# One weight buffer more, one load buffer less, and S5 steps held back during attention: a two-layer hybrid backbone on one core

## The chip, the cores and the metric

The kernel runs on 1 core of a Trainium2 chip. The metric is the device time of one execution in microseconds; shown are the median and the spread of several runs. One more execution was taken with the hardware profiler, and all rows below are of that one.

## The reference

One inference step of a hybrid backbone over two layers. 128 context tokens and 128 latent tokens run through the same weights, so the kernel treats them as 256 columns. For each layer:

```
mod = silu(cond) @ w_mod + b_mod                # six vectors of 2048, for context and for latent
h   = rms_norm(x) * (1 + scale1) + shift1
z   = h @ w_in      # q | k | v | rglru x | rglru gate | s5 input | three branch gates
A   = attention(q, k, v)                        # 8 heads, 2 kv heads, QK norm, rotary positions
B   = gelu(gate) * rg_lru(conv4(x))             # both directions
C   = glu(gelu(s5(u) + d*u))                    # complex diagonal scan, both directions, 64 groups
x  += gate1 * ((g0*(A@w_pa) + g1*(B@w_pr) + g2*(C@w_ps)) @ w_o)
a,b = rms_norm(x)*(1+scale2)+shift2 @ w_up
x  += gate2 * ((gelu(conv3(a)) * b) @ w_down)
```

All of it is in float32. The outputs are both token streams, the new keys and values, and the final states of the two recurrences.

## The kernel before, in words

Features lie on the 128 partitions, the 256 tokens along the free dimension. A weight matrix is cut into tiles that give 128 output features each; such a tile is one *item* of kind "w" in a list, with 2048 values per partition, loaded as two halves of 1024 (512 KB each).

**Precision.** TensorE multiplies in a rounded 32-bit form, so each half is split. `emit_split` (L192) copies the raw half into a high part on ScalarE (`whi`), and the closure `small` subtracts that from the raw half on VectorE (`wlo`). Activations are split too. For each 128 rows of the contraction `mmx` (L379) runs one matmul of the high weights over 512 columns (high and low activations) and one of the low weights over 256; a tile has 16 such pairs, in one PSUM bank of two. `joined` (L391) then copies half of the bank on ScalarE and adds the other half on VectorE (`pj`); that add empties the bank, and the tile's evacuation `evac` follows. `unit` (L362) makes such an item; `unit2` (L403) makes one whose two halves are two output tiles with a contraction of 1024, so it has two `pj` (the projections `w_pa`, `w_pr`, `w_ps` and the GLU).

**Buffers.** `emit_dma` (L153) issues a load on SyncE's queue (SP) into one of `NRAW` buffers "raw". Loads are issued in item order, and the program may emit one only when the load `NRAW` places before it has been used (L181). The scheduler below gives it a buffer that has come free, so it waits on the chip for that buffer's last reader. A raw weight half is free after its `wlo`; a raw modulation load after its matmul. In the startup the loads go round `NRAW` raw buffers and eight places in wide tiles that nothing else uses yet; in the feed-forward blocks two of five tiles use wide places E0 and F4 (L160). `whi` and `wlo` have `HLB` buffers each. `nhalf` counts halves that are split and not used up: `emit_split` refuses when it stands at `HLB`, and `spend` (L230), called after the first eight pairs of a tile, gives one back and lets `pump_split` (L299) emit the next. `pump_split` goes no farther than the next weight item. So with three, the second half of the next tile is emitted in the middle of the running tile.

**Modulation.** The 384 modulation loads are read once and multiplied by narrow float32 matmuls straight from the raw buffer (items of kind "mod", `mod_mm` L422, eight records each). 64 of them belong to the startup. The other 320 are spread over the weight items: `filler` adds `MODR[seg]` of a load for each tile and puts in a group of four when the credit reaches four. `seg` is 0 in layer 0 up to the last branch gates, 1 up to its feed-forward, 2 to 4 in the feed-forward of layer 0, 5 in layer 1. Asserts demand that each modulation vector is there before its use.

**Order of the work.** `run_items` (L285) walks through the items. At each weight item it emits loads, splits, the matmuls, the evacuation, and then `feed_att` (L257) and `feed` (L242), which run steps of generators: attention (`att_gen` L1091, one step at each `feed_att`, which also runs in the middle of a tile), the RG-LRU (`lru_gen`, at a rate `RLRU` per tile) and S5 (`s5_gen` L997, in layer 0 with `s5_prep`, which makes the tables). S5 goes last: it gets steps while the planner's clock of VectorE, `clock()`, is below its clock of TensorE, `pe`, plus `LEAD` of the layer (in ns). After each tile `run_items` sets the VectorE clock to at least `pe`, so `LEAD` works afresh for each tile. The planner's costs are the formulas in `tt`, `stt`, `mm` and others; the order they give is in the program, and the framework's scheduler may shift an instruction that is ready ahead of one that is not. Each engine has its own queue of instructions.

S5 starts when half of its input is there (L1253), attention after the value projection (L1328). `pa_begin` drains attention before the projection `w_pa`, and S5 is drained after ten of the sixteen tiles of the third branch gate (`GS0`).

Of the kernel before, what the change touches and what calls it, by code (L numbers as in the profile page):

```python
# [31 lines left out]


class Builder:
    LEAD = (3900, 2700)
    HLB = 3
    GS0 = 10
    PATIENCE = 3
    NRAW = 6
    AHEAD = 20  # L40
    MODR = (1.5, 0.6, 0.65, 0.65, 0.65, 1.2)
    RLRU = (1.9, 1.9)
    NE = (3, 3)
    PA = 1
# [108 lines left out]
    def emit_dma(self, i, extra):  # L153
# [15 lines left out]
        for h in range(len(self.raws.get(i, [])), 2 if w else 1):  # L169
            k = self.nboot % (self.NRAW + 8) - self.NRAW if it.get("boot") else -1  # L170
            if k >= 0:
# [8 lines left out]
            else:  # L180
                if len(self.ring) >= self.NRAW and self.ring[-self.NRAW] not in self.done:  # L181
                    return False
                self.ring.append((i, h))
                raw = self.st("raw", [1024], name="raw", bufs=self.NRAW)
            self.nboot += 1
# [6 lines left out]
    def emit_split(self, i, h):  # L192

        if self.nhalf == self.HLB:
            return False
        self.nhalf += 1
        hi = self.st("whi", [1024], F32R, name="whi", bufs=self.HLB)
        lo = self.st("wlo", [1024], F32R, name="wlo", bufs=self.HLB)
        raw = self.raws[i][h]
# [41 lines left out]

    def feed(self):  # L242

        for g in sorted(self.gens, key=lambda g: g[3] == "s5"):
            if g[3] == "att":
                continue
            s5 = g[3] == "s5"
            g[2] = 0 if s5 else g[2] + g[1]
            if g[4] is not None:
                g[4] += 1  # L250
            while g in self.gens and (self.clock() < self.pe + self.LEAD[self.lay] if s5 else g[2] >= 1):
                if g[4] is not None and g[4] < self.PATIENCE:
                    break
                g[2] -= 1
                self.step(g)
# [1304 lines left out]
    def filler(self, n):  # L1560
        self.credit += self.MODR[self.seg] * n
        while self.credit >= 4 and self.modq:
            self.credit -= 4
            for _ in range(4):
                it = self.modq.pop(0)
                it["ffn"] = self.ffn
                self.items.append(it)
# [135 lines left out]
```

## Time and profile before

| what | value |
|---|---|
| median of 3 runs | 3059.31 us (3058.38 to 3062.9) |
| the profiled execution | 3053.26 us, of it the span 3051.5 us |
| TensorE (PE) busy | 2946.8 us, 97% |
| VectorE (DVE) busy | 2259.1 us, 74% |
| ScalarE (ACT) busy | 1718.7 us, 56% |
| DMA | 723.64 MB, mean 237 GB/s |
| weight splits (`wlo`) | 896, 1095.2 us |
| modulation loads | 384 of 512 KB |

How to read it: all times are microseconds of the profiled execution, counted from its first instruction. A busy share is over the whole span and hides the stages: S5, attention and the RG-LRU run beside the input projection and the branch projections, from about 163 to 820 us in layer 0 and from 1630 to 2230 us in layer 1; the two feed-forward blocks lie behind these. A matmul's end is modelled, so PE busy is not PE at its peak. In a view of waits a row says which engine's instruction sat idle, what it waited for, the idle time in total, how often, and the longest.

### The profile page before, as it was taken

The page shows a single profiled execution, that of the slowest core. Times are in us where ns is not written, and L with a number is a line of the kernel's source. Part 1 is how long each engine was busy: PE and PEld are TensorE (multiplying, and loading weights), DVE is VectorE, ACT ScalarE, POOL GpSimd, SP SyncE. Part 2 cuts the span into 40 slices and gives each one's busy share as a digit, 9 for nine tenths or more (in the row PEclk, how much of TensorE's full clock was granted, in tenths as well). Part 3 has the DMA queues.
Part 4 walks back from the last instruction along what each step waited for, and adds up shares of the span by engine and source line. Part 5 has one row for each costly group of instructions (what it writes and reads, how often), then busy time and mean ns, then how long its engine had stood idle before and what let it go on. Part 6 is the DMA issues. An engine that isn't in the chain of part 4 may idle for free.

```text
span 3051.5 us, 53446 instructions
## 1 busy us (share of the span) xinstructions
PE 2946.8 (97%) x20833; PEld 2474.8 (81%) x20833; DVE 2259.1 (74%) x4000; ACT 1718.7 (56%) x2905; POOL 45.9 (2%) x87
## 2 busy tenths in 40 slices
PE   6899999999999999999999999999999999999999
PEld 4787778777888888888887878777788888888888
DVE  6498888889777878777668787787755777666665
ACT  4355667745456755445567556686345566544553
POOL 0000000000000000000000000000000000000000
PEclk9999999999999999999999999999999999999999
DMA  9866667677776777777776767777677656555553
GB/s 387 308 201 217 236 225 256 238 253 249 242 244 221 251 249 262 257 258 265 250 269 224 261 217 246 252 247 252 240 268 265 210 176 210 191 189 187 185 195 132
DMA packets 188637, 723.64 MB, mean 237 GB/s; under 512 B 21536, under 2 KB 22080, under 8 KB 179552
## 3 DMA queue, kind: packets, MB, share of 16 engines
q1 hardware_dynamic: 180432, 689.86, 66.2%
q0 software_dynamic: 7664, 28.27, 2.5%
q8 instruction: 164, 2.69, 0.3%
q10 hardware_dynamic: 288, 2.10, 0.2%
q14 instruction: 89, 0.73, 0.1%
HBM read 704.46 MB, written 15.68 MB: 236 GB/s over the span
## 4 chain that ended last, share of the span: by engine, by line
PE 68%; DVE 14%; DMA 8%; ACT 7%; issue 3%; ACTq 0%; DVEq 0%; SPq 0%
PE ps_mm L124 60%; DMA raw<-in_w_in 5%; DVE wlo L72 5%; ACT whi L116 3%; PE ps_md L124 3%; PE ps_aux L124 2%; DVE xs L1046 2%; PE ps_v L124 1%; ACT ltmp L112 1%; DMA raw<-in_w_pr 1%; DVE xs L72 1%; PE ps_y L124 1%; DVE pd L72 1%; DMA raw<-in_w_pa 1%; DVE pb L72 1%
## 5 line engine op out<-in xcount | busy, mean ns | idle before, releaser
L124 PE MATMUL ps_mm<-h,whi 128*128 128x512 f32 (+1 forms) x4976 | 1745.2, 395 | 34.5 <-DVE pj L72 26.0
L72 DVE TENSOR_TENSOR wlo<-raw,whi 128x1024 fp32r<-128x1024 f32 x896 | 1095.2, 1223 | 457.4 <-ACT whi L116 448.2
L124 PE MATMUL ps_mm<-h,wlo 128*128 128x256 f32 x4912 | 1342.3, 284 | 18.4 <-DVE wlo L72 18.0
L116 ACT CAST whi<-raw 128x1024 fp32r<-128x1024 f32 x896 | 939.7, 1049 | 544.7 <-PE ps_mm L124 236.6
L124 PEld LDWEIGHTS ps_mm<-h,whi 128*128 128x128 f32 x4976 | 925.8, 190 | 245.8 <-DVE pj L72 31.6
L124 PEld LDWEIGHTS ps_mm<-h,wlo 128*128 128x128 f32 x4912 | 934.6, 190 | 48.8 <-DVE wlo L72 25.8
L116 ACT COPY pj<-ps_mm 128x256 f32<-128x256 f32 x479 | 176.0, 368 | 500.5 <-PE ps_mm L124 499.8
L124 PE MATMUL ps_mm<-hid,whi 128*128 128x512 f32 x1024 | 354.9, 393 | 0.0
L72 DVE TENSOR_TENSOR pj<-ps_mm,pj 128x256 f32<-128x256 f32 x479 | 201.5, 421 | 205.6 <-ACT pj L116 204.9
L124 PE MATMUL ps_mm<-br,whi 128*128 128x512 f32 x896 | 322.8, 402 | 9.8 <-DVE pj L72 8.9
L124 PE MATMUL ps_mm<-hid,wlo 128*128 128x256 f32 x1024 | 277.2, 281 | 0.0
L124 PE MATMUL ps_mm<-br,wlo 128*128 128x256 f32 x896 | 233.4, 281 | 0.7 <-DVE wlo L72 0.6
L124 PEld LDWEIGHTS ps_mm<-hid,whi 128*128 128x128 f32 x1024 | 188.5, 188 | 39.6 <-issue 1.2
L124 PEld LDWEIGHTS ps_mm<-br,whi 128*128 128x128 f32 x896 | 165.5, 188 | 55.3 <-DVE pj L72 18.0
L124 PEld LDWEIGHTS ps_mm<-hid,wlo 128*128 128x128 f32 x1024 | 193.2, 189 | 5.1
L124 PEld LDWEIGHTS ps_mm<-br,wlo 128*128 128x128 f32 x896 | 169.0, 189 | 8.7 <-DVE wlo L72 1.0
L124 PE MATMUL ps_md<-raw,SC 128*32 128x256 f32 x2560 | 160.8, 382 | 0.0
L124 PEld LDWEIGHTS ps_md<-raw,SC 128*32 128x32 f32 x2560 | 78.7, 110 | 56.3 <-issue 15.1
L112 ACT ACT_TABLE_LOAD x81 | 103.9, 1283 | 10.1 <-DMA cv<-in_cT 5.2
L112 ACT ACTIVATE RH<-CST,TINY 128x256 f32<-128x256 f32 x128 | 57.9, 500 | 63.4 <-DVE xs L1046 63.4
L1046 DVE TENSOR_TENSOR_SCAN xs<-RH,xs 128x1056 f32<-128x1056 f32 x32 | 75.3, 2355 | 0.7
L85 DVE SCALAR_TENSOR_TENSOR x<-pj,MOD,x 128x128 f32<-128x128 f32 x192 | 59.0, 349 | 3.1
(239 smaller groups left out, 2434.1 us busy)
## 6 DMA issues: line engine op xcount, KB each, us to landing
raw<-in_w_mod SPq DMA_DIRECT2D x384, 512.0 KB, 6.8
raw<-in_w_in SPq DMA_DIRECT2D x304, 512.0 KB, 4.8
raw<-in_w_up SPq DMA_DIRECT2D x168, 512.0 KB, 4.3
raw<-in_w_down SPq DMA_DIRECT2D x90, 512.0 KB, 4.4
raw<-in_w_up SPq DMA_DIRECT2D x44, 1024.0 KB, 4.8
raw<-in_w_o SPq DMA_DIRECT2D x64, 512.0 KB, 4.4
raw<-in_w_down SPq DMA_DIRECT2D x19, 1024.0 KB, 4.8
raw<-in_w_pa SPq DMA_DIRECT2D x32, 512.0 KB, 4.6
```

The source lines that it names most:

```text
L72: self.nc.vector.tensor_tensor(out=out, in0=a, in1=b, op=op)
L85: self.nc.vector.scalar_tensor_tensor(out=out, in0=a, scalar=s, in1=b, op0=op0, op1=op1)
L112: self.nc.scalar.activation(out, a, func, **k)
L116: self.nc.scalar.copy(out, a)
L124: self.nc.tensor.matmul(out, lhsT, rhs, start=start, stop=stop, **k)
L1046: nc.vector.tensor_tensor_scan(out=x, data0=r, data1=x, initial=0.0, op0=ALU.mult, op1=ALU.add)
```

## The change

`HLB` goes from 3 to 4, so `whi` and `wlo` have four buffers each. `NRAW` goes from 6 to 5. `LEAD` goes from 3900 to 4700 ns in layer 0 and from 2700 to 3300 ns in layer 1, and a new `LEADA` of 1000 ns takes its place in `feed` while an attention generator is alive. `MODR` is 1.3 instead of 1.5 and 1.0 instead of 1.2 in segments 0 and 5, and 0.8 instead of 0.6 to 0.65 in the others. What is computed stays the same.

```diff
--- before.py
+++ after.py
@@ -32,13 +32,14 @@
 
 
 class Builder:
-    LEAD = (3900, 2700)
-    HLB = 3
+    LEAD = (4700, 3300)
+    LEADA = 1000
+    HLB = 4
     GS0 = 10
     PATIENCE = 3
-    NRAW = 6
+    NRAW = 5
     AHEAD = 20
-    MODR = (1.5, 0.6, 0.65, 0.65, 0.65, 1.2)
+    MODR = (1.3, 0.8, 0.8, 0.8, 0.8, 1.0)
     RLRU = (1.9, 1.9)
     NE = (3, 3)
     PA = 1
@@ -241,14 +242,16 @@
 
     def feed(self):
 
+        att = any(g[3] == "att" for g in self.gens)
         for g in sorted(self.gens, key=lambda g: g[3] == "s5"):
             if g[3] == "att":
                 continue
             s5 = g[3] == "s5"
+            lead = self.LEADA if att else self.LEAD[self.lay]
             g[2] = 0 if s5 else g[2] + g[1]
             if g[4] is not None:
                 g[4] += 1
-            while g in self.gens and (self.clock() < self.pe + self.LEAD[self.lay] if s5 else g[2] >= 1):
+            while g in self.gens and (self.clock() < self.pe + lead if s5 else g[2] >= 1):
                 if g[4] is not None and g[4] < self.PATIENCE:
                     break
                 g[2] -= 1
```

## Rows read from the trace of the kernel before

**Rows 1.** The page's head and part 1: span; busy us, share, instructions

```profile
span 3051.5 us, 53446 instructions
...
PE 2946.8 (97%) x20833; PEld 2474.8 (81%) x20833; DVE 2259.1 (74%) x4000; ACT 1718.7 (56%) x2905; POOL 45.9 (2%) x87
```

**Rows 2.** The chain of waits in its last stretch: start us, us, what

```profile
2540.30 507.00 PE ps_mm L124 x2911
```

**Rows 3.** TensorE's waits, whole span: engine line waited for: us, times, longest

```profile
PE ps_mm L124 <- DVE pj L72: 34.9, 29, 4.2
PE ps_mm L124 <- DVE wlo L72: 18.5, 19, 3.6
...
PE ps_mm L124 <- ACT whi L116: 8.5, 11, 1.7
PE ps_aux L128 <- DVE rkc L100: 7.3, 2, 3.7
```

**Rows 4.** TensorE's waits, 0 to 163 us, the startup

```profile
PE ps_mm L124 <- DVE wlo L72: 6.6, 6, 3.6
PE ps_mm L124 <- ACT whi L116: 4.7, 7, 1.1
```

**Rows 5.** TensorE's waits, 163 to 820 us, layer 0 with S5

```profile
PE ps_mm L124 <- DVE pj L72: 18.8, 11, 4.2
```

**Rows 6.** TensorE's waits, 1630 to 2230 us, layer 1 with S5

```profile
PE ps_mm L124 <- DVE pj L72: 13.1, 9, 3.9
```

**Rows 7.** Windows: stretch, us, busy of PE, PEld, DVE, ACT, POOL, clock, DMA

```profile
312.00:500.00 188.00, 177.18 (x1431) 145.49 (x1430) 163.58 (x296) 126.85 (x205) 5.37 (x10) 0.98 0.68 232
1830.00:2005.00 175.00, 168.06 (x1256) 139.51 (x1255) 133.68 (x199) 118.31 (x192) 2.69 (x5) 1.00 0.73 252
```

**Rows 8.** Windows of the tile wlo alone: busy of PE, PEld and DVE

```profile
312.00:500.00 188.00, 100.62 (x373) 71.59 (x372) 56.07 (x46) 0.98 0.68 232
```

**Rows 9.** ScalarE's waits, whole span

```profile
ACT whi L116 <- PE ps_mm L124: 236.6, 188, 6.2
ACT whi L116 <- DMA raw<-in_w_in: 154.5, 108, 6.7
```

**Rows 10.** ScalarE's waits, 163 to 820 us

```profile
ACT whi L116 <- DMA raw<-in_w_in: 63.6, 45, 6.7
...
ACT whi L116 <- PE ps_mm L124: 32.8, 17, 4.9
```

**Rows 11.** VectorE's waits, whole span

```profile
DVE wlo L72 <- ACT whi L116: 448.2, 456, 4.4
```

**Rows 12.** Timeline of TensorE: a modulation group and the tile behind it

```profile
392.97 1.91 PE L124 MATMUL ps_md<-raw,SC 128*32 128x256 f32 x32
394.81 0.50 PE L124 MATMUL ps_mm<-br,whi 128*128 128x512 f32 x1
```

**Rows 13.** Timeline of all engines, 384 to 391 us: start us, us, engine, line

```profile
384.09 0.33 SPq L186 DMA_DIRECT2D raw<-in_w_pa  x1
...
386.49 1.22 DVE L72 TENSOR_TENSOR wlo<-raw,whi 128x1024 fp32r<-128x1024 f32 x1
...
387.73 2.74 SPq L186 DMA_DIRECT2D raw<-in_w_in  x2
387.81 1.05 ACT L116 CAST whi<-raw 128x1024 fp32r<-128x1024 f32 x1
...
388.89 1.23 DVE L72 TENSOR_TENSOR wlo<-raw,whi 128x1024 fp32r<-128x1024 f32 x1 [0.52 <-ACT whi L116]
...
390.22 0.37 ACT L116 COPY pj<-ps_mm 128x256 f32<-128x256 f32 x1 [1.36 <-PE ps_mm L124]
...
390.63 0.42 DVE L72 TENSOR_TENSOR pj<-ps_mm,pj 128x256 f32<-128x256 f32 x1 [0.51 <-ACT pj L116]
```

**Rows 14.** Windows of the tile ps_md alone: busy of PE, PEld, DVE, ACT

```profile
163.00:820.00 657.00, 58.21 (x902) 29.13 (x902) 1.13 (x6) 2.50 (x7) 0.99 0.70 236
1630.00:2380.00 750.00, 61.24 (x968) 30.77 (x968) 1.63 (x8) 1.46 (x4) 0.99 0.72 250
```

## The prediction

> **What bounds the kernel now.** I began with the page's head and its busy line [rows 1]: TensorE is busy for 2946.8 of 3051.5 us, so about 104.7 us are all that any cover of waits can win back. The work itself (448 weight tiles, 384 modulation loads, the S5 matmuls) is the same after the change. The chain of waits shows what a tile costs when nothing disturbs it: in the last stretch 2911 matmuls, 32 to a tile, take 507.00 us, 5.57 us a tile [rows 2]. The chain's DVE and DMA shares elsewhere are not idle TensorE, only the path that happened to arrive last; so the next view was TensorE's own waits [rows 3]. There are few: 34.9 us for the sum that empties a PSUM bank (pj), 18.5 us for the low half of a split weight (wlo), 8.5 us for the high half (whi), 7.3 us for the key norms that open attention (rkc). Cut by stretch, 11.3 us of wlo and whi lie in the startup [rows 4]; of pj, 18.8 us lie in layer 0 while S5 runs [rows 5] and 13.1 us in the same stretch of layer 1 [rows 6]. The two feed-forward blocks have next to none. So the change can matter in some 1250 us, where VectorE carries split, evacuation and S5 steps in one order.
>
> There VectorE is nearly full in layer 0 and not in layer 1: 163.58 us of 188 against 133.68 of 175 [rows 7]. 46 wlo in the first [rows 8], and as many in the second, are 23 tiles, so 7.11 and 5.81 us of VectorE work a tile; the tile's period is 8.17 us in layer 0, and less TensorE's idle 10.82 us (0.47 a tile) it would be 7.70.
>
> **The change, part by part.** Sums are made against the profiled execution, 3053.26 us (1.76 more than its span); the median of the runs is 6.05 above that, and I add it at the end.
>
> Fourth split buffer. With three, the second half of the next tile is split only when TensorE has spent the first half of the running one. With four it may be split half a tile (2.8 us) earlier, and a wait that comes from this gate goes. What it can win is bounded by the 27.0 us of wlo and whi waits [rows 3] and by 0. ScalarE's waits before whi say how much of it is the gate: 236.6 us until TensorE, 154.5 us until a load of the input projection [rows 9]; in layer 0's S5 stretch it is the other way round, 32.8 against 63.6 [rows 10]. I take half: -13.5. VectorE also stops blocking: it sat 448.2 us before wlo until whi [rows 11], with S5 steps and pj queued behind it. Where it runs late it then catches up, so I take a quarter of the pj waits, -9; ends -17 (half) and, as two wlo now can stand ahead of a pj, 32 two-result tiles at up to 0.3 us, +10.
>
> Attention hold. With LEADA at 1000 hardly an S5 step follows a tile while attention lives, as its evacuation and softmax already use that lead. The two waits for rkc are 7.3 us [rows 3]; part of each is its own square root, reciprocal and transpose. I take -4; ends 0 and -7.3.
>
> More lead elsewhere. After each tile the planner fills VectorE until it stands LEAD ahead of TensorE, so 0.8 us more in layer 0 and 0.6 in layer 1 is a larger share per tile, not a larger stock. Layer 0: 7.11+0.8=7.91 us against a tile that needs 7.70; the lower MODR takes 0.2 load a tile away, a quarter of 1.91 us each [rows 12], 0.10, so 7.60. VectorE is over by 0.31 us for some 50 tiles until S5 ends: up to 16 us of new pj waits, less what the fourth buffer gives it back. I take +6; ends 0 and +16. Layer 1: 5.81+0.6=6.41 stays below its period of 7.61: 0. S5 ends earlier in both, and nothing waited for that. Its steps issue DMAs too: tables on POOL's queue in layer 0, blocks on SP's in layer 1, a few tiles later or earlier in either; POOL is idle and SP's are 24 among some 1200: 0.
>
> Five raw buffers. Four modulation loads are issued far ahead of their matmuls and sit in their buffers; before, two buffers went round for weights in that time, now one. One round trip, from issue to the low half, was 6.0 us: issue at 384.09, whi at 387.81, wlo at 388.89 for 1.23; and a load reuses a buffer as soon as its wlo ends (387.71, next issue 387.73) [rows 13]. The tile after a modulation group has two halves, which now come one after the other: 12.1 us from the end of the split before them. The time for it is two tiles, the group (1.91 and some 0.3 to get in) and half a tile, 2.5x5.57+2.2=16.1 us in a calm stage, so that split must end 4.0 us into its tile. In VectorE's queue stand before it, in a tile: 0.41 us until the bank's copy is there (390.22 to 390.63) [rows 13], all its work but the splits, which was 7.11-2.46=4.65 in layer 0 and 5.81-2.46=3.35 in layer 1 and grows by 0.8 and 0.6, and the two wlo themselves (2.46): 8.3 us and 6.8 us. S5's own matmuls lengthen the two tiles by 2x(7.60-5.57-0.72)=2.6 us, with 0.72 for the group spread over its 3.08 tiles. So the half is up to 1.7 us late in layer 0 and 0.2 in layer 1. Groups are 32 records: 902/32=28 in layer 0's stretch and 968/32=30 in layer 1's [rows 14]; at the new rates 24 and 25. The ends are 0 and 24x1.7+25x0.2=+46. The total of weight halves held, five raw and four split against six and three, is the same nine, and an earlier split frees its raw buffer earlier; so I take 0.2 us a group, nearer to nothing: +10. In the pair of loads shown, a start at 384.09 would still give the second half at 396.2, and TensorE reached the second half of the tile behind that group, begun at 394.81 [rows 12], after about 397.6: hidden by 1.4 us. Where it is not hidden, ScalarE's pj copy stands behind the waiting whi, VectorE's pj and S5 steps behind its wlo, and on SP's queue the next loads; TensorE waits for pj then.
>
> The Trainium skill, Perfetto Trace Analysis, section Optimization Strategy, says that the same gap repeating on the engine that should be full can mean that there is no room for the next tile's buffer. By that one adds to the buffer that is waited for, and in layer 0's S5 stretch [rows 10] that is the raw load, of which the change takes one away; it speaks for the slower rival below.
>
> The Trainium skill, DMA: Bandwidth & Descriptors, section Anatomy of one DMA, gives about 2.0 us fixed plus bytes at 436 GB/s, measured on another queue; for 512 KB an estimate of 3.2 us. The row has at most 3.72 (384.09 to 387.81). By the Trainium skill the two trips are about 11.1 us and the lateness in layer 0 is 0.7 us instead of 1.7.
>
> The moved modulation groups are the same 80 and cost the same where they land: 0. One load fewer in flight at the start: 0, ends -2 and +3, as the boot loads also use eight wide places.
>
> Sum: -13.5-9-4+6+10=-10.5, so 3042.8 for a profiled execution and 3048.8 for the median.
>
> **The rivals.** First, forecast: waits for splits and attention shrink, the lead and the raw buffer give part back; 3048.8, its own range 3034 to 3053.
> Second, slower: the single raw buffer beside four parked modulation loads. Place: the second half of the first tile after each group, in both S5 stretches. Price +46; with only the split's -13.5 and attention's -4 beside it +28.5, 3088 at its worst. It decides from (13.5+9+4-6)/49=0.42 us a group on; at twice that, 0.8 a group, the net is 49x0.8-20.5=+18.7, 3078, which I take. For it: ScalarE waits for loads rather than for TensorE in layer 0 [rows 10]. Against: the example is hidden.
> Third, slower: VectorE full in layer 0. +16 for the lead, +5 raw, -6 split, -4 attention: 3070. For it 7.91 over 7.60; against, S5 ends earlier and the tiles after it have VectorE free.
> Fourth, nothing: a wait removed at wlo is taken up at pj, since both stand behind the same VectorE work: 3059. For it: with VectorE at 87%, many pj waits come with no idle VectorE before them.
> Fifth, more: -20 split, -14 pj, -6 attention, +2 lead, +3 raw: 3024. For it the ceiling of 104.7; against, TensorE's waits must nearly vanish.
>
> **How the numbers follow.** Forecast 0.38, second 0.25, third 0.10, fourth 0.17, fifth 0.10. What a measurement of this kernel can tell is about 0.2%, 6 us. Faster is forecast and fifth, 0.48; same 0.17; slower 0.35. The range from 3018 to 3088 reaches over the fifth (3024) and to the second's worst (3088); a fuller win and a worse queue stay out.
>
> **What would show it.** TensorE's waits until wlo and whi should fall from 27.0 to about 14 us, those until pj from 34.9 to about 32 (less nine, plus six of lead), and the two for rkc from 7.3 to about 3. ScalarE's wait before whi until TensorE falls, that until loads rises. VectorE's share in layer 0 after attention should rise above 0.90, and the last S5 scan should come some 40 us earlier. I am wrong if TensorE's idle time after modulation groups grows by more than 0.4 us each, with whi waiting for a load there, or if wlo and whi waits stay and pj grows.

## The result: slower, and the profile after

The changed kernel takes 3100.38 us (median of 4 runs, 3097.25 to 3103.51) against 3058.85 for the kernel before: ratio 1.0132, 95% interval 1.0116 to 1.0147. The forecast was 3048.8 and its range ended at 3088; the time lies outside, on the side of the second rival.

The page's head and busy line, as in [rows 1]:

```profile
span 3095.5 us, 52977 instructions
...
PE 2965.0 (96%) x20833; PEld 2479.8 (80%) x20833; DVE 2254.8 (73%) x4000; ACT 1727.3 (56%) x2909; POOL 45.9 (1%) x87
```

The counts of TensorE and VectorE are those of before, so their work is the same. Of the 44.0 us by which the span grew, 25.8 are idle TensorE (130.5 us against 104.7) and 18.2 are matmuls that show as longer, by their modelled ends. The chain's last stretch is untouched, 507.00 us for 2911 matmuls as in [rows 2]:

```profile
2583.93 507.00 PE ps_mm L125 x2911
```

All was lost ahead of it. TensorE's waits, whole span (waiting instruction <- what it waited for: us, times, longest us), the answer to [rows 3]; in this kernel L73, L117 and L125 are the helpers that were L72, L116 and L124:

```profile
PE ps_mm L125 <- DVE wlo L73: 38.4, 50, 2.1
PE ps_mm L125 <- ACT whi L117: 21.7, 22, 2.9
PE ps_mm L125 <- DVE pj L73: 17.2, 15, 3.9
...
PE ps_aux L129 <- DVE attf L91: 7.4, 5, 2.8
PE ps_aux L125 <- DVE kv L73: 2.7, 1, 2.7
```

The order has turned round. Waits for the two halves of a split weight went from 27.0 to 60.1 us and from 30 times to 72; waits for pj halved, from 34.9 to 17.2. By stretch the largest part is layer 0 with S5, where [rows 5] had pj on top (163 to 820 us again; in this kernel the same work ends some 17 us later):

```profile
PE ps_mm L125 <- DVE wlo L73: 15.4, 16, 1.9
PE ps_mm L125 <- ACT whi L117: 7.2, 6, 2.2
PE ps_mm L125 <- DVE pj L73: 5.0, 4, 3.7
```

ScalarE, which makes whi out of the raw load, points to the reason. First its waits over the whole span [rows 9], then over 163 to 820 us [rows 10]:

```profile
ACT whi L117 <- DMA raw<-in_w_in: 191.4, 135, 4.7
ACT whi L117 <- PE ps_mm L125: 100.4, 93, 1.8
...
ACT whi L117 <- DMA raw<-in_w_down: 37.7, 22, 5.0
ACT whi L117 <- DMA raw<-in_w_pr: 36.1, 23, 3.8
ACT whi L117 <- DMA raw<-in_w_up: 33.4, 18, 4.0
```

```profile
ACT whi L117 <- DMA raw<-in_w_in: 78.1, 59, 4.7
ACT whi L117 <- DMA raw<-in_w_pr: 28.3, 14, 3.8
```

The wait until TensorE (the gate of the split buffers) fell from 236.6 to 100.4 us. Part of that is the fourth split buffer's doing, part only the late loads: with five raw and three split buffers, a run below, it is 163.0. The waits until a load rose, from 154.5 to 191.4 for the input projection and for three other weights as well (w_down had 12.9 before, w_pr 23.0, w_up 7.4): the split is allowed earlier and finds no raw data. SyncE's queue says who holds the raw buffers: its waits until a modulation group's matmuls went from 74.8 us, 93 times, to

```profile
SPq L187 <- PE ps_md L125: 173.6, 143, 8.5
```

One group of layer 0 shows the whole course. First the loads on SyncE's queue (start us, us, queue, line, what, how many), of narrow windows, as a wide one merges neighbours:

```profile
475.71 12.52 SPq L187 DMA_DIRECT2D raw<-in_w_mod  x4
489.00 0.33 SPq L187 DMA_DIRECT2D raw<-in_w_in  x1
...
496.08 0.33 SPq L187 DMA_DIRECT2D raw<-in_w_in  x1
497.61 1.94 SPq L187 DMA_DIRECT2D raw<-in_w_in  x4
```

and then the timeline of the engines (in brackets the idle time before an instruction and what ended it):

```profile
493.75 1.05 ACT L117 CAST whi<-raw 128x1024 fp32r<-128x1024 f32 x1 [1.98 <-DMA raw<-in_w_in]
...
494.82 1.22 DVE L73 TENSOR_TENSOR wlo<-raw,whi 128x1024 fp32r<-128x1024 f32 x1 [0.49 <-ACT whi L117]
...
496.94 1.91 PE L125 MATMUL ps_md<-raw,SC 128*32 128x256 f32 x32
...
498.77 0.50 PE L125 MATMUL ps_mm<-h,whi 128*128 128x512 f32 x1
...
501.54 0.28 PE L125 MATMUL ps_mm<-h,wlo 128*128 128x256 f32 x1
501.69 1.04 ACT L117 CAST whi<-raw 128x1024 fp32r<-128x1024 f32 x1 [4.69 <-DMA raw<-in_w_in]
...
502.77 1.23 DVE L73 TENSOR_TENSOR wlo<-raw,whi 128x1024 fp32r<-128x1024 f32 x1 [1.50 <-ACT whi L117]
...
502.79 0.50 PE L125 MATMUL ps_mm<-h,whi 128*128 128x512 f32 x1 [0.98 <-ACT whi L117]
...
504.05 0.44 PE L125 MATMUL ps_mm<-h,wlo 128*128 128x256 f32 x1 [0.76 <-DVE wlo L73]
...
504.29 0.63 PE L125 MATMUL ps_mm<-h,whi 128*128 128x512 f32 x1
```

Four modulation loads, issued from 475.71 on, sit in four raw buffers until their matmuls at 496.94. The fifth buffer serves the tile behind the group alone: its first half is issued at 489.00 and split by 496.04 (494.82 + 1.22); only then, at 496.08, goes the second. TensorE begins the tile at 498.77 and reaches the second half behind the matmul of 501.54; there it stands 0.98 us for whi and 0.76 for wlo. Then the granted clock halves, as the windows show (stretch, us, busy of PE, PEld, DVE, ACT, POOL, clock, DMA share, GB/s):

```profile
498.00:504.20 6.20, 4.47 (x34) 3.04 (x27) 4.67 (x12) 2.48 (x3) 0.24 (x1) 1.00 0.92 301
504.20:507.60 3.40, 3.40 (x12) 2.92 (x13) 3.37 (x5) 3.14 (x4) 0.00 (x0) 0.51 0.95 372
```

For all such places I took the start of every matmul of a trace and summed the gaps over 0.4 us beyond the usual distance of that pair, sorted by the time since the last modulation group began. (Another way of pairing the matmuls moves such a sum by some 3 us.) Between 3 and 8 us after one, where the second half of the next tile is due, the kernel before has none behind its 80 groups; the changed one has 35, 39.1 us in all: 14 in layer 0's S5 stretch (17.9 us), 8 in layer 1's (8.5), 13 elsewhere (12.8). 31 of the 35 end when whi or wlo is there. All other gaps after the startup stayed about as they were in sum, 67.7 us before and 65.0 after.

That sum hides a second place. Sorted by the matmul instead of by time, and only where whi or wlo ended the wait, the first two matmuls of the second half of the tile behind a group have 33 gaps, 34.6 us (none before), and the first two of the tile after that have 18, 24.2 us (6 and 5.7 us before). So the shortage runs on into the next tile, while pj waits shrank.

Stretches at about half the granted clock are 48.9 us of the span before and 72.2 after. Behind the startup they are 9.7 us longer (the other 13.6 lie in the startup, where TensorE has idle time anyway); if half of such a stretch is lost matmul time, that is an estimate of 4.9 us. The gaps there grew by 36.4 us (39.1 - 2.7), and the startup ends 2.2 us later (the first tile behind it starts at 166.92 us instead of 164.68). These are 43.5 of the 44.0 us, as near as such a count can come.

### The profile page after: what moved, and what is told of

It reads as the page before. It is cut to its first block, busy times and chain, and to the rows that moved or that the text cites. A ratio compares the mean times of both kernels' runs of the same rounds, so it can differ in the third digit from the quotient of the medians.

```text
span 3095.5 us, 52977 instructions
## 1 busy us (share of the span) xinstructions
PE 2965.0 (96%) x20833; PEld 2479.8 (80%) x20833; DVE 2254.8 (73%) x4000; ACT 1727.3 (56%) x2909; POOL 45.9 (1%) x87
## 4 chain that ended last, share of the span: by engine, by line
PE 65%; DMA 12%; DVE 11%; ACT 7%; issue 5%; SPq 0%; POOL 0%; ACTq 0%; DVEq 0%; POOLq 0%
PE ps_mm L125 57%; DMA raw<-in_w_in 8%; DVE wlo L73 5%; ACT whi L117 3%; PE ps_md L125 3%; PE ps_aux L125 2%; PE ps_v L125 1%; DMA raw<-in_w_pa 1%; PE ps_y L125 1%; DVE xs L1049 1%; ACT ltmp L113 1%; DMA raw<-in_w_o 1%; DVE pj L73 1%; DMA raw<-in_w_pr 1%; DVE xs L73 1%
## 5 line engine op out<-in xcount | busy, mean ns | idle before, releaser
L125 PE MATMUL ps_mm<-h,whi 128*128 128x512 f32 (+1 forms) x4976 | 1743.7, 395 | 31.0 <-ACT whi L117 17.9
L73 DVE TENSOR_TENSOR wlo<-raw,whi 128x1024 fp32r<-128x1024 f32 x896 | 1090.6, 1221 | 429.4 <-ACT whi L117 424.0
L125 PE MATMUL ps_mm<-h,wlo 128*128 128x256 f32 x4912 | 1344.9, 284 | 31.8 <-DVE wlo L73 30.4
L117 ACT CAST whi<-raw 128x1024 fp32r<-128x1024 f32 x896 | 937.3, 1049 | 529.6 <-DMA raw<-in_w_in 191.4
L125 PEld LDWEIGHTS ps_mm<-h,whi 128*128 128x128 f32 x4976 | 924.4, 189 | 239.5 <-ACT whi L117 24.5
L125 PEld LDWEIGHTS ps_mm<-h,wlo 128*128 128x128 f32 x4912 | 933.5, 190 | 72.0 <-DVE wlo L73 46.7
L117 ACT COPY pj<-ps_mm 128x256 f32<-128x256 f32 x479 | 176.0, 368 | 526.5 <-PE ps_mm L125 525.3
L73 DVE TENSOR_TENSOR pj<-ps_mm,pj 128x256 f32<-128x256 f32 x479 | 200.9, 420 | 251.0 <-ACT pj L117 249.9
L125 PE MATMUL ps_mm<-hid,whi 128*128 128x512 f32 x1024 | 355.6, 393 | 1.4 <-ACT whi L117 1.4
L125 PE MATMUL ps_mm<-br,whi 128*128 128x512 f32 x896 | 324.9, 405 | 9.1 <-DVE pj L73 6.3
L125 PE MATMUL ps_mm<-hid,wlo 128*128 128x256 f32 x1024 | 277.6, 281 | 1.8 <-DVE wlo L73 1.8
L125 PE MATMUL ps_mm<-br,wlo 128*128 128x256 f32 x896 | 237.3, 285 | 7.4 <-DVE wlo L73 6.2
L125 PEld LDWEIGHTS ps_mm<-hid,whi 128*128 128x128 f32 x1024 | 188.6, 188 | 41.9 <-ACT whi L117 2.0
L125 PEld LDWEIGHTS ps_mm<-br,whi 128*128 128x128 f32 x896 | 167.1, 191 | 51.8 <-DVE pj L73 10.6
L125 PEld LDWEIGHTS ps_mm<-hid,wlo 128*128 128x128 f32 x1024 | 193.2, 189 | 7.7 <-DVE wlo L73 2.7
L125 PEld LDWEIGHTS ps_mm<-br,wlo 128*128 128x128 f32 x896 | 171.5, 191 | 19.4 <-DVE wlo L73 9.9
L125 PE MATMUL ps_md<-raw,SC 128*32 128x256 f32 x2560 | 158.4, 381 | 0.0
L125 PEld LDWEIGHTS ps_md<-raw,SC 128*32 128x32 f32 x2560 | 79.1, 109 | 54.2 <-issue 14.9
L113 ACT ACTIVATE RH<-CST,TINY 128x256 f32<-128x256 f32 x128 | 58.9, 501 | 28.9 <-DVE xs L1049 28.8
L86 DVE SCALAR_TENSOR_TENSOR fa<-pj,PK,fa 128x254 f32<-128x254 f32 x120 | 57.5, 479 | 5.7 <-ACT fa L113 4.0
```

The costliest lines, as they stand in the source:

```text
L73: self.nc.vector.tensor_tensor(out=out, in0=a, in1=b, op=op)
L86: self.nc.vector.scalar_tensor_tensor(out=out, in0=a, scalar=s, in1=b, op0=op0, op1=op1)
L113: self.nc.scalar.activation(out, a, func, **k)
L117: self.nc.scalar.copy(out, a)
L125: self.nc.tensor.matmul(out, lhsT, rhs, start=start, stop=stop, **k)
```

## The experiments

Each time is a median and each ratio stands against the kernel before on the same chip, whose median was 3056.69 to 3060.22 us in these runs. The reordering below is one edit to `run_items`; it asks for the weight loads of the tile behind a modulation group ahead of the group's own loads. Some expectations name a run by its number: e6 is the change reordered, e11 seven raw buffers reordered with old settings, e12 five raw and four split buffers reordered with old settings.

```diff
+        for k in range(n - 1):
+            if items[k]["kind"] == "mod" and items[k + 1]["kind"] == "w" and not items[k].get("boot"):
+                p = loads.index(k + 1)
+                q = p
+                while q and items[loads[q - 1]]["kind"] == "mod":
+                    q -= 1
+                loads.insert(q, loads.pop(p))
```

| raw / split buffers, settings of LEAD, LEADA, MODR | us | ratio, 95% interval |
|---|---|---|
| 6/3, old (before) | 3056.69 to 3060.22 | 1 |
| 5/4, new (the change) | 3100.38 | 1.0132 [1.0116, 1.0147] |
| 5/4, old | 3107.00 | 1.0169 [1.0145, 1.0194] |
| 6/3, new | 3057.57 | 0.9996 [0.9986, 1.0005] |
| 5/3, old | 3151.77 | 1.0305 [1.0282, 1.0329] |
| 7/3, old | 3020.26 | 0.9869 [0.9855, 0.9884] |
| 5/4, new, reordered | 3044.75 | 0.9960 [0.9945, 0.9975] |
| 6/3, old, reordered | 3040.06 | 0.9935 [0.9920, 0.9950] |
| 5/4, old, reordered | 3060.76 | 0.9999 [0.9983, 1.0015] |
| 5/3, old, reordered | 3077.16 | 1.0054 [1.0038, 1.0070] |
| 7/3, old, reordered | 3013.41 | 0.9865 [0.9851, 0.9878] |
| 7/3, new, reordered | 3029.82 | 0.9916 [0.9903, 0.9928] |
| 6/3, LEAD alone new | 3053.71 | 0.9990 [0.9980, 1.0000] |
| 6/3, LEADA alone added | 3054.57 | 1.0002 [0.9990, 1.0014] |

**Which part of the change: the buffers alone, and the order alone.** Against the kernel before:

```diff
-    HLB = 3
+    HLB = 4
-    NRAW = 6
+    NRAW = 5
```

> The kernel before with four split buffers and five raw buffers, everything else as before. Theory A (the raw buffer that was given up is what costs: with four modulation loads parked, weight halves come one after another): nearly the whole slowdown is here, 3088 to 3105 us, and TensorE's waits for whi and wlo go from 27 to 50 us or more, most of them 5 to 11 us after a modulation group begins. Theory B (the larger lead fills VectorE in layer 0): 3045 to 3060 us, whi and wlo waits no larger than before.

Measured 3107.00, 1.0169. The buffers alone cost as much as the whole change, by the medians 7 us more; the two intervals touch. TensorE's waits have the same new order:

```profile
PE ps_mm L124 <- DVE wlo L72: 41.6, 51, 2.4
PE ps_mm L124 <- ACT whi L116: 35.4, 34, 2.6
...
PE ps_mm L124 <- DVE pj L72: 13.9, 11, 6.9
```

The other half, against the changed kernel:

```diff
-    HLB = 4
+    HLB = 3
-    NRAW = 5
+    NRAW = 6
```

> The changed kernel with the buffers of before (three split, six raw): only LEAD, LEADA and MODR are changed. Theory A: 3050 to 3068 us, whi and wlo waits of TensorE near 27 us. Theory B: 3080 us or more, with pj waits in layer 0 above 18.8 us.

Measured 3057.57, 0.9996 with an interval that holds 1. The order settings as a set are worth nothing here with the old buffers; they move waits about (pj 34.9 to 27.7, rkc 7.3 to 1.3, wlo 18.5 to 24.0).

**Which buffer: five raw ones alone, seven alone.**

```diff
-    NRAW = 6
+    NRAW = 5
```

> The kernel before with five raw buffers instead of six, three split buffers kept. Theory A: slower than with four split buffers, as one half less is held in all: 3100 us or more, +40 or more. If instead the fourth split buffer is what hurts (its order on VectorE), this stays within 3059 +-10.

Measured 3151.77, 1.0305: the lost raw buffer by itself costs 92 us, and between this and the buffers alone the fourth split buffer gives 45 back. The gaps 3 to 8 us behind a group are 65 here, 69.9 us. TensorE's waits:

```profile
PE ps_mm L124 <- ACT whi L116: 49.8, 53, 2.8
PE ps_mm L124 <- DVE wlo L72: 44.6, 59, 2.7
PE ps_mm L124 <- DVE pj L72: 18.2, 18, 3.8
```

The opposite edit takes the same room as the change (a split buffer is a whi and a wlo, two raw buffers' worth, so seven raw and three split take what five raw and four split take):

```diff
-    NRAW = 6
+    NRAW = 7
```

> The kernel before with seven raw buffers instead of six, nothing else. Theory A1 (what costs is one thing only, that the two halves behind a modulation group go round in a single buffer): with six buffers they already had two, so a seventh gives little, 3050 to 3060 us. Theory A2 (every raw buffer counts, since ScalarE waits for loads all along): another step down of 15 us or more, below 3045.

Measured 3020.26, 0.9869. So 5, 6 and 7 raw buffers with three split ones give 3152, 3059 and 3020. With seven, ScalarE's waits before whi are headed by TensorE, and the wait until a load of the input projection has fallen from 154.5 to 17.3 us:

```profile
ACT whi L116 <- PE ps_mm L124: 298.6, 217, 4.6
ACT whi L116 <- issue: 86.8, 49, 5.7
...
ACT whi L116 <- DMA raw<-in_w_in: 17.3, 13, 5.7
```

**Why: the parked loads.** If the loss comes from four parked modulation loads that leave one buffer for weights, then it must go when the weights are asked for first, with all buffers as they are in the change. The reordering, put into the changed kernel:

> The changed kernel, with one thing moved: the loads of the weight tile behind a modulation group are issued before the four loads of that group instead of behind them, so that these two halves no longer have to go round in the one raw buffer beside the parked loads. Same loads, same matmuls in the same order. Theory A: most of the 41 us come back, 3055 to 3075 us, and the waits 5 to 7 us after a group begins vanish. Theory B: stays at 3095 to 3105 us.

Measured 3044.75, 0.9960 where the change has 1.0132: 53 us came back by order of issue alone. The gaps 3 to 8 us behind a group fall from 35 to 5 (39.1 to 6.6 us); of the waits for whi or wlo, one gap is left in the second half of the tile behind a group (33 before the reordering) and none at the start of the tile after it (18). The waits for whi and wlo fall to less than before the change (19.5 us against 27.0), and pj is first again. SyncE's wait until a group's matmuls is no smaller for it (193.6 us where the change has 173.6), so that row alone did not show the cost. And the group now waits for its own load, a little:

```profile
PE ps_mm L125 <- DVE pj L73: 36.0, 24, 4.4
...
PE ps_mm L125 <- DVE wlo L73: 11.7, 10, 3.6
...
PE ps_mm L125 <- ACT whi L117: 7.8, 10, 1.6
PE ps_md L125 <- DMA raw<-in_w_mod: 3.5, 2, 2.5
```

The same edit on the kernel before:

> The kernel before, with the loads of the weight tile behind a modulation group issued ahead of the group's loads. Theory A1: little to gain with six buffers, 3050 to 3060 us, as TensorE has no waits 3 to 8 us after a group there. Theory A2: below 3045 us.

Measured 3040.06, 0.9935. Before had no gap 3 to 8 us behind a group, yet gained 20 us: wlo went from 18.5 to 13.8, pj from 34.9 to 28.6, and gaps 8 to 13 us behind a group, a tile later, from 42.9 to 35.2. That suggests that two buffers beside the parked loads were not quite enough either.

On the buffers alone (`HLB = 4`, `NRAW = 5`) and on five raw ones alone (`NRAW = 5`), old settings:

> Four split buffers and five raw buffers with LEAD and MODR of before (3107 us without the reordering), and the loads reordered. Theory A: 3040 to 3060 us. What is then below the kernel before is the worth of the fourth split buffer; what is above e6's 3045 us the worth of the lead, the hold and the modulation rates.

> Five raw buffers, three split buffers, LEAD and MODR of before (3152 us without the reordering), loads reordered. Theory A: falls by 70 us or more, to 3060 to 3080 us; the rest over e12 is the fourth split buffer. If the single round-trip buffer were not the cause, the reordering would leave it above 3130 us.

Measured 3060.76 (0.9999) and 3077.16 (1.0054); by the ratios 52 and 77 us came back, and the gaps 3 to 8 us behind a group fell to 3.0 and 8.6 us. With the reordering the fourth split buffer is worth 16 us (3077.16 to 3060.76, same chip).

The fair comparison, reordered against reordered (3040.06, same chip), says how much is not the order of issue. One raw buffer fewer still costs 37 us, where it cost 92; one raw buffer fewer for one split buffer more still costs 21 us, where it cost 47.5. So the weights that came too late behind a parked group make somewhat over half of the loss, and the rest stays when they are asked for first. Where it lies is only partly seen: with five raw and three split buffers TensorE waits 9.0 us for the groups' own loads, a row that the six do not have, and pj is 36.5 us against 28.6; with five and four pj is 46.0, and the stretches at half clock behind the startup are 58.9 us against 23.9.

**Towards the best version.** Seven raw buffers and the reordering with the old settings, and the same with the change's settings:

```diff
-    NRAW = 6
+    NRAW = 7
...
+    LEAD = (4700, 3300)
+    LEADA = 1000
+    MODR = (1.3, 0.8, 0.8, 0.8, 0.8, 1.0)
```

(The lower three lines stand in the second of the two alone, with the lines of `feed` that use `LEADA`; the reordering, as above, in both.)

> The kernel before with seven raw buffers and the reordered loads, which alone gave -40 and -20 us. If both cure the same late loads: 3012 to 3022 us, little under seven buffers alone. If they were two causes the gains would add to about 3000 us.

> The same with LEAD, LEADA and MODR of the changed kernel. With loads in time, what is left are pj waits of VectorE's own backlog. If the larger lead costs as I had it (+6) and the hold in attention gives 4: within 6 us of e11. A gain of over 10 us would say that these settings were good and only hidden by the load waits.

Measured 3013.41 (0.9865), the fastest of the study and ahead of both kernels, and 3029.82 (0.9916). The reordering on top of the seventh buffer is not shown to add anything: the ratios 0.9865 and 0.9869 have overlapping intervals, as they would if both edits cure the same thing. The order settings cost 16 us here; of the waits that grew, the largest is that of the groups for their loads, not among the leading rows in the other kernel (whi and wlo together grew from 17.6 to 22.7, and pj fell from 20.6 to 14.7):

```profile
PE ps_md L125 <- DMA raw<-in_w_mod: 9.0, 5, 4.0
```

while with five raw and four split buffers, reordered, they gained (0.9960 against 0.9999, intervals apart). Which of LEAD, LEADA and MODR does either is open; MODR was not run alone.

**The two disputed terms of the order.** LEAD alone, then LEADA alone, on the kernel before:

```diff
-    LEAD = (3900, 2700)
+    LEAD = (4700, 3300)
```

> The kernel before with LEAD of the changed kernel alone, 4700 and 3300 ns. My term for it was +6 us, bounds 0 and +16, by pj waits in layer 0: 3060 to 3076 us. If VectorE is not filled up by it: within 3 us of before.

Measured 3053.71, 0.9990 with an interval that ends at 1. VectorE in the window of [rows 7] (there 163.58):

```profile
312.00:500.00 188.00, 178.88 (x1452) 147.40 (x1451) 162.42 (x300) 124.35 (x199) 4.84 (x9) 0.97 0.68 236
```

```diff
+        att = any(g[3] == "att" for g in self.gens)
...
+            lead = 1000 if att else self.LEAD[self.lay]
...
-            while g in self.gens and (self.clock() < self.pe + self.LEAD[self.lay] if s5 else g[2] >= 1):
+            while g in self.gens and (self.clock() < self.pe + lead if s5 else g[2] >= 1):
```

> The kernel before with S5 steps held back in attention (LEADA 1000), LEAD and MODR as before. My term was -4 us, bounds 0 and -7.3, out of TensorE's waits for rkc, 7.3 us before: 3052 to 3059 us, rkc waits about 3 us. S5 gets its steps later then, so pj waits behind attention may grow instead.

Measured 3054.57, 1.0002, and the waits for rkc did not fall (7.3 to 9.1 us).

## Why the prediction was wrong, step by step

**Where it failed.** The step is "Five raw buffers": "The total of weight halves held, five raw and four split against six and three, is the same nine, and an earlier split frees its raw buffer earlier; so I take 0.2 us a group, nearer to nothing: +10." The count of nine is right and says nothing, for in the group shown four of the raw buffers hold modulation loads for up to 21 us (475.71 to 496.94), and a split buffer cannot hold those. Left for weights are one raw buffer against two. In the changed kernel the gaps behind the groups are 26.4 us over the 46 groups of the two S5 stretches, 0.57 a group, past the 0.42 at which the same text had the balance turn there. Over all 80 it is 0.49, past the 0.4 that the text named as a sign of being wrong. The mechanism, its place (second half of the tile behind a group) and its sign (whi waiting for a load) were written down as the second rival; the choice between its bounds was the error: +10 stood where the raw buffer taken by itself measured +92.

**Why even its worst, 3088, was too low.** The worst case was 46 us of lateness, less 13.5 for the split buffer and 4 for attention. The lateness itself did not break its bound: layer 0 came to 0.72 us a group (17.9 over 25) where 1.7 was the bound, layer 1 to 0.40 (8.5 over 21) where 0.2 was. That 0.2 holds a slip: the 2.6 us by which S5's matmuls lengthen two tiles are layer 0's. By layer 1's own row [rows 7] a tile needs 168.06/23 = 7.31 us, 7.21 with the lower MODR; less 5.57 and 0.55 for the group over its four tiles that is 2.2 us for two tiles, and the bound comes to 0.6. The round trip, taken as 6.0 us from [rows 13], was 7.0 us for the first half in the timeline above (489.00 to 496.04) and 7.9 for the second (496.08 to 504.00), the latter beside four loads issued between 497.61 and 499.55.

What the worst case lacked lies elsewhere. Neither credit came, as the waits for whi and wlo rose and attention's moved on. 13 of the 35 gaps lie outside the S5 stretches, where I had put nothing (12.8 us). The lateness went on into the tile after, as waits for whi and wlo (24.2 us against 5.7); the text put no price on that and named pj, which fell by 17.7 us and took part of the loss back. And there is the half clock, an estimated 5 us behind the startup.

**The hint in the rows.** ScalarE waited 63.6 us for loads against 32.8 for TensorE in layer 0 [rows 10]: the raw buffer was the one that was short. I had it as evidence for the rival and gave it 0.25. The pair of loads that I held against it was hidden by 1.4 us in the kernel before; it was one pair in a calm place, and the trips of 7.0 and 7.9 us above take more than these 1.4 us away. The Trainium skill, Perfetto Trace Analysis, section Optimization Strategy, says that the same gap repeating on the engine that should be full can mean missing room for the next tile; here the trace agrees, with 33 gaps for whi or wlo at the same two matmuls, and 40 us won by a seventh raw buffer.

**Fourth split buffer.** -13.5 and -9 were put down. It is worth 45 us beside five raw buffers and 16 with the loads reordered there: right in sign and, in the second case, near in size; beside six raw buffers it was not measured. ScalarE's wait until TensorE fell as forecast. But beside five raw buffers the waits until wlo and whi rose to 60.1 instead of falling to 14, since the gate was replaced by the load. pj fell much further than to 32, to 17.2, but not by VectorE catching up: with the loads reordered it is 36.0 us in the changed kernel, and with old settings 46.0 with four split buffers against 36.5 with three. So the -9 is not borne out; it fits that TensorE stood earlier, at the split.

**Attention hold.** rkc fell from 7.3 to 0.2 us, as its sign said, but attf rose from 2.6 to 7.4 and kv brought 2.7: the wait moved on, and -4 was not there. LEADA alone did nothing.

**More lead.** +6 did not show. LEAD alone cannot be told from no change; VectorE's work in the window of layer 0 did not rise (162.42 us against 163.58), and the last S5 scan came at 734.7 instead of 773.2 us: S5 ended 38 us earlier in that kernel, as the sign said, without VectorE's share rising. In the changed kernel the share was 0.81, not above 0.90, and the scan came at 767.7:

```profile
312.00:504.00 192.00, 179.42 (x1441) 145.62 (x1439) 155.33 (x289) 127.38 (x203) 5.37 (x10) 0.99 0.64 220
```

With 45 wlo in it, 22.5 tiles, that is 6.90 us of VectorE work a tile where 7.91 was worked out. The planner fills until a lead in time, and stalled loads delay it as well; the third rival is out, as pj in layer 0 fell to 5.0 us.

**Moved modulation groups, one load fewer at the start.** 0 each. The startup stretch up to 163 us has TensorE busy 126.9 us against 125.8 and ends 2.2 us later, inside the range given for it. The groups' share was not isolated.

**The sum.** With the measured parts it reads: raw buffer +92, fourth split buffer -45, and -6 left for the order settings beside these buffers (41.5 for the change against 47.5 for the buffers alone; the intervals of the two ratios touch): +41.5. With the old buffers the order settings gave -2, within what can be told from no change. My -10.5 had the split buffer near its size in the reordered kernels, if for a reason (pj) that they do not show, and the raw buffer at a ninth of its own.

## What to carry to other kernels

Count a pool of buffers by what is parked in it: the number that matters is what is left for the stream while the longest-held tenants sit there, and buffers of the next stage do not replace it. Before giving room to a buffer, read which wait ends last ahead of the instruction that fills it (here ScalarE's wait for a load, not for TensorE): the room that cost 42 us in the change won 40 as a seventh raw buffer. A transfer shown as just hidden has no slack to give, and issuing what is needed soon ahead of what will be parked can win a good part of what another buffer wins (77 of 92 us with five raw buffers, 20 of 40 with six).

## What the runs showed of the hardware

A short wait of TensorE can have a second price. In the group shown the matmuls at 502.79 and 504.05 start 1.25 and 1.26 us behind the ones before them; then the granted clock goes from 1.00 to 0.51 (2.4 to 1.2 GHz) for the window shown, in which the 128x512 matmul takes 0.63 us instead of 0.39. Inside the span such stretches are 48.9 us before, 72.2 after, and 83.8 and 88.7 in the two kernels with five raw buffers and the old settings. In the changed kernel ten of them lie behind the startup, and eight follow closely on such a gap; but of its 48 gaps over 1 us most were not followed by one, and what decides it no run here shows.

The load of one weight half was longer beside others: from issue to the start of whi 4.75 us at 489.00 and 5.61 us at 496.08, against at most 3.72 in [rows 13].
